# Latent attention on one core: the maxima's pieces moved between the scores, a narrower turn, and the gates applied after the heads

## The chip, the cores and the metric

The kernel runs on one core of a Trainium2 chip, in one launch. The metric is device time in microseconds (us), the median of several runs. The core's engines work side by side and wait for each other through semaphores: TensorE (PE in the profile, its weight loads PEld), VectorE (DVE), ScalarE (ACT), GpSimd (POOL) and SyncE (SP), which here issues nearly all DMAs. TensorE writes into PSUM, eight banks of 128 partitions by 512 float32.

## What is computed

The reference is a two-layer backbone: a layer of windowed attention, a layer of latent attention, and a last RMSNorm. There are 1024 latent tokens and 256 context tokens, so 1280 keys. The change touches the second layer only, from its attention on:

```python
s = (einsum("bqhd,bkhd->bhqk", qn, kn) + einsum("bqhd,bkd->bhqk", qr, kr)) * scale
p = softmax(s, axis=-1)
o = einsum("bhqk,bkhd->bqhd", p, v)          # 16 heads of 64
yx = (o * silu(gx)) @ w_out                  # the gate, then the output projection
x = x + gate_x * yx                          # then the final RMSNorm
```

## The kernel before

**Units.** The attention is cut into 16 units (`UnitB`, L1276; `NU = 16`): a unit is a pair of heads and one half (512) of the queries. Units 0 and 1 are the halves of pair 0, and so on. Its ten key tiles of 128 tokens are numbered c = 0 to 9.

**Scores and exponentials.** `score(c)` (L1332) multiplies key tile c with the unit's queries, keys on the partitions and 512 queries in the columns. The two heads lie in the two 64-row halves of the array and run side by side, so a "pair" of matmuls is two that overlap. There are five such pairs for each c: four with operands split into high and low parts (terms 0 to 3) and a fifth with 36 rows (term 4), in which four extra rows subtract the row maximum of each query. `score(c, i0, i1)` issues only terms i0 to i1. When the fifth is issued, ScalarE's exponential over both heads' banks follows (L1347), then an add of the result to a running sum (L1351, L1353; on GpSimd, and on VectorE for c > 4 of the last unit). The bank pair is 3,4 for even c and 5,6 for odd c, so S2, the scores of c = 2, can be written only when the exponential of c = 0 has read its banks. In what follows S2 is a tile's scores and E2 its exponential.

**Maxima.** Before unit u+1 can start, the row maxima of its scores must be known. They are taken from a rougher product with the queries on the partitions: `top(piece)` (L1297) issues four matmuls (eight of half the width for two of the ten pieces), and VectorE reduces each of two banks to a maximum (L1311, L1313). The ten pieces T0 to T9 of unit u+1 are issued within unit u. Their banks are 0, 1 and 2, taken in turn, two for a piece; so the second matmul of a piece waits for the reduction of the first bank of the piece before it. T4 and T9 are the two of eight matmuls.

**Turn and shift.** `turn` (L1315) reduces the pieces' maxima to one for each query and transposes them on TensorE, one 128-row by 100-column transpose (L1318). `shift` (L1320) writes them in diagonal form into the extra rows of the queries: for one head on VectorE (L1323), for the other as four ScalarE instructions (L1330).

**PV, and the end of a unit.** `PV` (L1355) multiplies the exponentials with the values, five key tiles at a time, into bank 7. `fin` copies the result out and loads the unit's gate; `fin2` adds the running sums over the partitions by a matmul with ones into bank 5 (L1371) and copies them out on ScalarE (L1373); `fin3(j)` takes the reciprocal of half the columns and multiplies (L1377, L1378); `fin4` multiplies with the gate and stores to DRAM (L1382, L1384). They run a unit late: unit u's `fin2` stands in unit u+1.

**Order.** In this part of the kernel the order on each engine is the order in which the program is written (`in_order`). For a unit the loop L1506 to L1556 issues:

```
S0 terms 0-3, S1 terms 0-3, T0, S0 term 4, T1, S1 term 4, S2, T2, S3, T3, S4, T4,
[fin2 of the last unit, PV of c = 0..4, fin3(0) of the last unit],
S5, T5, S6, T6, S7, T7, S8, T8, S9, T9, PV of c = 5..9, turn, fin3(1), shift, fin4, fill, fin
```

The fill is the next pair's keys (`make_K`, after units 0, 2, 4 up to 12), or the next four heads' values (`make_V`, after units 3, 7 and 11). After units 1, 5, 9, 13 and 14 there is none, so the next unit's S0 follows the turn at once.

**Queues.** SyncE's queue holds the loads of queries for the unit after next (`prep`, L1288), the gate's load, the stores of `fin4` and some loads of the output weights; it works in order too.

**Output tiles.** After the units, `out_tiles` (L1426) makes eight tiles of 128 tokens: 48 matmuls each (two halves of the columns, eight k-steps, three products: L126 to L128), four PSUM banks in turn. In tile t, after the first 24 matmuls, `cut_out` splits the attention output of tile t+1 into high (ScalarE, L121) and low part (VectorE, L122), and `fetch_out` (L1411) loads that of tile t+2. VectorE then multiplies with the layer's gate vector and adds x (L1447, L1448), ScalarE squares (L1449), GpSimd makes the root of the mean in three small instructions (L1459 to L1461), VectorE scales (L1472), SyncE stores (L1473). The first two fetches and the first cut stand in the last unit.

Of the kernel before, what the change touches and what calls it, by code (L numbers as in the profile page):

```python
# [22 lines left out]
NT = TOK // 128  # L23
# [36 lines left out]
def kernel(ctx: ExitStack, tc: tile.TileContext, t, out, dbg=None):  # L60
    nc = tc.nc
# [57 lines left out]
    def split(hi, lo, src, lo_eng=None):  # L119

        nc.scalar.copy(hi, src)  # L121
        (lo_eng or nc.vector).tensor_sub(lo, src, hi.bitcast(F32))  # L122
# [498 lines left out]
    units = [UnitA(ti, g) for ti in ORDER for g in range(4)]  # L621
# [43 lines left out]
    aw, xn, hs, w0 = {}, {}, {}, {}  # L665
# [201 lines left out]
    for bi, gp, c in order:  # L867
# [18 lines left out]
        r = proj_t(bi, gp, c)  # L886
# [22 lines left out]
    og = None  # L909
    fins = []  # L910
    for ui, u in enumerate(units):
# [248 lines left out]
    for ti in range(NT):  # L1160
        n = ti + 3
# [45 lines left out]
    NU = 16  # L1207
# [6 lines left out]
    glr = Ring(R, [30, 112], 512)  # L1214
# [61 lines left out]
    class UnitB:  # L1276
# [38 lines left out]
        def turn(self, bank):  # L1315
            nc.vector.reduce_max(shp(self.mx, 2, 64)[:, :, 32:36], self.mxp, AX.X, negate=True)
            self.pm = bank
            nc.tensor.transpose(self.pm[0:100, 0:128], self.mx[:, 0:100], ident)  # L1318

        def shift(self, engs):  # L1320
            for r, eng in zip((slice(32, 36), slice(96, 100)), engs):
                if eng is nc.vector:
                    eng.tensor_tensor(  # L1323
                        shp(self.q[r, 3], 4, 128), self.pm[r, 0:128].unsqueeze(1).to_broadcast([4, 4, 128]),
                        ident[r, r].unsqueeze(2).to_broadcast([4, 4, 128]), ALU.mult,
                    )
                else:
                    for b in range(4):
                        o = self.q[r, 3, b * 128 : b * 128 + 128]
                        eng.activation(o, self.pm[r, 0:128], AF.Copy, scale=ident[r, r.start + b : r.start + b + 1])  # L1330

        def score(self, c, i0=0, i1=5):  # L1332


            q, kt = self.q, self.kt
            cs = slice(c * 128, c * 128 + 128)
            b = 3 + 2 * (c % 2)
            terms = ((kt, 0, 0, 64), (kt, 0, 1, 64), (kt, 1, 0, 64), (KR, 0, 2, 64), (KR, 1, 3, 36))
            for i in range(i0, i1):
                k, s, sq, n = terms[i]  # L1340
                for e in range(2):
                    r = slice(64 * e, 64 * e + n)
                    nc.tensor.matmul(PB[:, b + e, :], k[r, s, cs], q[r, sq], start=i == 0, stop=i == 4)  # L1343
            if i1 < 5:
                return
            E = self.E[c] = shp(Er.next(), 2, 512)
            nc.scalar.activation(E, PB[:, b : b + 2, :], AF.Exp)  # L1347
            acc = shp(self.acc, 2, 512)
            eng = nc.vector if self.i == NU - 1 and c > 4 else nc.gpsimd
            if c == 1:  # L1350
                eng.tensor_add(acc, self.E[0], E)  # L1351
            elif c:
                eng.tensor_add(acc, acc, E)  # L1353
# [8 lines left out]
        def fin(self):  # L1362
            self.o = otr.next()
            nc.scalar.copy(self.o, PB[:, 7, :])
            self.gt = glr.next()
            load(out=self.gt.bitcast(F32), in_=g1_d[self.pair, :, self.ts])

        def fin2(self):
            acc = shp(self.acc, 2, 512)
# [2 lines left out]
            self.rec = self.acc[:, 0:512]  # L1372
            nc.scalar.copy(self.rec, psd)  # L1373

        def fin3(self, j):
            js = slice(256 * j, 256 * j + 256)
            nc.vector.reciprocal(self.rec[:, js], self.rec[:, js])  # L1377
            nc.vector.tensor_mul(self.o[:, js], self.o[:, js], self.rec[:, js])  # L1378
# [10 lines left out]
    ogl = Ring(R, [114, 118], 1024)  # L1389
    xr1 = Ring(R, [122, 126, 130], 1024)  # L1390
    yr = Ring(F, [26, 10, 14], 1024)
    junk1 = f_at(8, 256).bitcast(BF16)
# [16 lines left out]
                yield  # L1409

    def fetch_out(ti):  # L1411
        o = shp(ogl.next(), 8, 128)
        load(out=o.bitcast(F32), in_=og_d[:, :, ti * 128 : ti * 128 + 128].rearrange("c p n -> p c n"))
        x = xr1.next().bitcast(F32)
        load(out=x, in_=x1_d[256 + ti * 128 : 384 + ti * 128, :])
        return o, x

    def cut_out(f, eng=None):
        o, x = f
        og = shp(ogr1.next(), 2, 8, 128)  # L1420
        for h in range(2):
            hs = slice(4 * h, 4 * h + 4)
            split(og[:, 0, hs], og[:, 1, hs], o[:, hs].bitcast(F32), eng)
        return og, x

    def out_tiles(ready, got):  # L1426
# [66 lines left out]
    for b in range(4):  # L1493
        for i in range(3):
            units[0].top([(b, i)], (PB[:, 2 * i, :], PB[:, 2 * i + 1, :]))
        next(gs[b])
        next(gs[b])
        if b == 3:
            units[0].turn(psd)
            units[0].shift((nc.vector, nc.vector))  # L1500
# [5 lines left out]
    for ui, u in enumerate(units):  # L1506
        pu = units[ui - 1] if ui else None
        nu = units[ui + 1] if ui + 1 < NU else None
        nnu = units[ui + 2] if ui + 2 < NU else None
        for c in range(NT):  # L1510
            if c == 5:
                if pu:
                    pu.fin2()
                u.PV(0, 5)
                if pu:
                    pu.fin3(0)
                if pu and nu is None:
                    pu.fin4(0, 256)
                    first = fetch_out(0)
                    pu.fin3(1)  # L1520
                    pu.fin4(256, 512)
                    got = fetch_out(1)
            if c == 0:
                u.score(0, 0, 4)
                u.score(1, 0, 4)
            if c > 1:
                u.score(c)
            if nu:
                nu.top(PIECES[c])
            if c < 2:  # L1530
                u.score(c, 4, 5)
            if 0 < ui < 12 and c == 2 or ui == 6 and c == 7 or ui in (12, 13) and c in (2, 7):
                next(wo_fill, None)
            if nu is None and c == 0:
                load2(out=gx1, in_=gate_d[1, 0, :].partition_broadcast(128))
                load2(out=fg, in_=t["final_g"].partition_broadcast(128))
        if nnu:
            nnu.prep()
        u.PV(5, NT)
        if nu:  # L1540
            filled = u.half == 0 and u.pair < 7 or ui % 4 == 3
            nu.turn(psd if filled else topb())
            if pu:
                pu.fin3(1)
            nu.shift((nc.vector, nc.scalar))
            if pu:
                pu.fin4()
            fillb.i = topb.i
            fill = make_K(u.pair + 1) if u.half == 0 and u.pair < 7 else iter(())
            if ui % 4 == 3:  # L1550
                fill = make_V(ui // 4 + 1)
            for _ in fill:
                pass
        else:
            ready = cut_out(first)
        u.fin()  # L1556
    u.fin2()
    u.fin3(0)
    u.fin3(1)
    u.fin4()  # L1560
    out_tiles(ready, got)
    in_order.__exit__(None, None, None)

# [74 lines left out]
```

## Time and profile before

| | us |
|---|---|
| median of 3 runs | 1582.75 |
| lowest, highest | 1579.58, 1583.51 |
| the profiled execution's own time | 1582.15 |
| its span, first to last instruction | 1580.3 |
| TensorE busy in the span | 1522.8 |
| VectorE, GpSimd, ScalarE busy | 1015.2, 775.4, 734.9 |

The profile is of one execution. Rows of the timeline give start, duration, engine, line, operation, shapes, how many equal instructions were merged into the row, and in brackets the idle time before it with what ended it. A matmul's duration includes its way through the array (0.39 us for 512 columns), while the next starts 0.23 us later; so steps are read from start to start. The units lie between 1002.5 us (first turn) and 1485.8 us (first output matmul); the output tiles follow, to about 1573 us on TensorE.

### The profile page before, as it was taken

To read this page: it belongs to the slowest core of one execution; us is meant where nothing else is said; L and a number is where in the kernel's file an instruction comes from. 1 tells how busy PE (TensorE), PEld (TensorE's weight loads), DVE (VectorE), ACT (ScalarE), POOL (GpSimd) and SP (SyncE) were. 2 spreads that over 40 slices of the span, in tenths; PEclk is the share of its full clock that TensorE was granted. 3 is DMA by queue.
4 is the path that set the end of the run, shared out by engine and by line. 5 is a ranking of instruction groups with operands and counts; after the bars stand their busy time and mean duration, and the time that the engine had idled before them with its cause. 6 is when DMAs were issued, how large, how long until landed. Compare 5 with 4: busy or idle time off the path is not lost.

```text
span 1580.3 us, 24759 instructions
## 1 busy us (share of the span) xinstructions
PE 1522.8 (96%) x9026; PEld 1189.2 (75%) x9026; DVE 1015.2 (64%) x1895; ACT 734.9 (47%) x1433; POOL 775.4 (49%) x722
## 2 busy tenths in 40 slices
PE   6899999989999999998999999999999999999998
PEld 2788888778888888886987888766766666766687
DVE  2666868737767887777725202567678678677644
ACT  2512212238877777776523432344445444544422
POOL 2653446315554434444318340477677677688200
PEclk8999999989999999999999999999999999999999
DMA  8535644473333333316304841401122112111442
GB/s 301 175 118 183 196 144 171 144 223 108 114 111 94 97 94 94 94 55 222 92 16 145 308 129 54 117 15 50 44 68 71 44 44 87 44 45 37 140 160 80
DMA packets 123842, 178.91 MB, mean 113 GB/s; under 512 B 11708, under 2 KB 71996, under 8 KB 123720
## 3 DMA queue, kind: packets, MB, share of 16 engines
q1 hardware_dynamic: 116440, 166.40, 33.2%
q10 hardware_dynamic: 7280, 10.92, 2.3%
q8 instruction: 71, 1.16, 0.3%
q14 instruction: 51, 0.42, 0.1%
HBM read 131.13 MB, written 46.15 MB: 112 GB/s over the span
## 4 chain that ended last, share of the span: by engine, by line
PE 83%; DVE 5%; DMA 3%; POOL 3%; issue 3%; ACT 3%; SPq 0%; POOLq 0%; DVEq 0%; ACTq 0%
PE PB L126 14%; PE PB L127 13%; PE PB L128 13%; PE PB L1343 12%; PE PB L1360 9%; PE PB L1305 5%; PE PB L570 5%; PE PB L560 4%; PE PB L533 2%; PE PB L534 2%; PE PB L1371 1%; DMA arena_f<-a_w_in 1%; DMA arena_f<-x 1%; DVE arena_f L344 1%; POOL arena_r L122 1%
## 5 line engine op out<-in xcount | busy, mean ns | idle before, releaser
L126 PE MATMUL PB<-arena_r 128*128 128x512 f32 (+2 forms) x1312 | 475.7, 363 | 3.4 <-ACT arena_r L205 2.1
L127 PE MATMUL PB<-arena_r 128*128 128x512 f32 (+2 forms) x1312 | 469.5, 358 | 3.2 <-POOL arena_r L727 2.3
L128 PE MATMUL PB<-arena_r 128*128 128x512 f32 (+2 forms) x1312 | 469.2, 358 | 0.2 <-DVE arena_r L122 0.2
L1353 POOL TENSOR_TENSOR arena_f<-arena_f 128x1024 f32<-128x1024 f32 x123 | 294.6, 2395 | 18.8 <-ACT arena_f L1347 11.6
L126 PEld LDWEIGHTS PB<-arena_r 128*128 128x128 f32 x1312 | 250.4, 191 | 48.2 <-issue 6.9
L127 PEld LDWEIGHTS PB<-arena_r 128*128 128x128 f32 x1312 | 249.9, 191 | 37.8 <-POOL arena_r L727 2.8
L128 PEld LDWEIGHTS PB<-arena_r 128*128 128x128 f32 x1312 | 249.6, 190 | 35.4 <-DVE arena_r L122 0.4
L1311 DVE TENSOR_REDUCE krF<-PB 128x1 f32<-128x512 f32 (+1 forms) x264 | 167.2, 678 | 112.2 <-PE PB L1305 111.8
L1347 ACT ACTIVATE arena_f<-PB 128x1024 f32<-128x1024 f32 x160 | 164.3, 1027 | 157.2 <-PE PB L1343 154.5
L1343 PE MATMUL PB<-arena_r 64*128 64x512 f32 (+1 forms) x1600 | 220.0, 395 | 1.0 <-ACT arena_f L1347 0.9
L122 POOL TENSOR_TENSOR arena_r<-arena_f,arena_r 128x512 fp32r<-128x512 f32 x96 | 131.5, 1382 | 166.7 <-ACT arena_r L121 152.8
L1343 PEld LDWEIGHTS PB<-arena_r 64*128 64x128 f32 (+1 forms) x1600 | 159.4, 184 | 41.5 <-issue 13.3
L122 DVE TENSOR_TENSOR arena_r<-PB,arena_r 128x512 fp32r<-128x512 f32 (+2 forms) x215 | 140.1, 663 | 76.8 <-ACT arena_r L121 75.1
L540 DVE CUSTOM_DVE_ANT_0 arena_f<-PB,arena_f,small 128x256 f32<-128x256 f32 (+1 forms) x288 | 145.4, 524 | 32.6 <-PE PB L534 25.7
L121 ACT CAST arena_r<-PB 128x512 fp32r<-128x512 f32 (+2 forms) x215 | 120.0, 565 | 55.2 <-PE PB L560 40.9
L1360 PE MATMUL PB<-arena_f 128*64 128x512 f32 x640 | 143.6, 595 | 0.0
L541 ACT ACTIVATE arena_f<-arena_f,small 128x640 f32<-128x640 f32 (+2 forms) x160 | 118.9, 743 | 27.8 <-DVE small L540 26.7
L570 PE MATMUL PB<-arena_r 128*128 128x512 f32 x336 | 121.8, 438 | 4.7 <-ACT arena_f L581 4.1
L344 DVE SCALAR_TENSOR_TENSOR arena_f<-arena_f,small 128x512 f32<-128x512 f32 x98 | 116.2, 1232 | 3.9 <-DMA arena_f<-ada_w 3.5
L1305 PE MATMUL PB<-arena_r 64*128 64x512 f32 (+1 forms) x768 | 112.3, 360 | 6.5 <-DVE krF L1311 5.8
L1360 PEld LDWEIGHTS PB<-arena_f 128*64 128x64 f32 x640 | 44.4, 137 | 84.3 <-issue 82.0
L560 PE MATMUL PB<-ident,arena_f 128*128 128x128 f32 x672 | 105.8, 274 | 0.4 <-ACT arena_f L541 0.3
(165 smaller groups left out, 1892.8 us busy)
## 6 DMA issues: line engine op xcount, KB each, us to landing
arena_r<-q_d SPq DMA_DIRECT2D x148, 128.0 KB, 2.8
arena_f<-ada_w SPq DMA_DIRECT2D x64, 256.0 KB, 3.2
arena_f<-a_w_in SPq DMA_DIRECT2D x40, 256.0 KB, 3.0
arena_f<-ada_w SPq DMA_DIRECT2D x16, 512.0 KB, 7.2
arena_f<-x SPq DMA_DIRECT2D x16, 512.0 KB, 3.7
q_d<-arena_f SPq DMA_DIRECT2D x16, 512.0 KB, 3.2
qn_d<-arena_f SPq DMA_DIRECT2D x16, 512.0 KB, 5.7
arena_r<-qn_d SPq DMA_DIRECT2D x16, 512.0 KB, 5.8
```

Of the source, the lines that this page charges most:

```text
L122: (lo_eng or nc.vector).tensor_sub(lo, src, hi.bitcast(F32))
L126: nc.tensor.matmul(o, ah, bh, start=first, stop=False)
L127: nc.tensor.matmul(o, al, bh, start=False, stop=False)
L128: nc.tensor.matmul(o, ah, bl, start=False, stop=last)
L560: nc.tensor.transpose(pt[:, h, :], self.Ps[h][:, ci * 128 : ci * 128 + 128], ident)
L570: nc.tensor.matmul(self.pv, V[:, self.chunks[ci], self.g, :], PT[:, s], start=ci == 0 and s == 0, stop=ci == self.m - 1 and s == 1,)
L1305: nc.tensor.matmul(bank[:, o : o + n], self.q[r, s, bs], k[r, 0, n0 : n0 + n], start=s == 0, stop=s == 2)
L1311: nc.vector.reduce_max(self.mxp[:, e, b : b + 1, i], bank[:, 0:n], AX.X)
L1343: nc.tensor.matmul(PB[:, b + e, :], k[r, s, cs], q[r, sq], start=i == 0, stop=i == 4)
L1347: nc.scalar.activation(E, PB[:, b : b + 2, :], AF.Exp)
L1353: eng.tensor_add(acc, acc, E)
L1360: nc.tensor.matmul(PB[r, 7, :], Vq[:, c, h, :], E[:, e], start=c == 0, stop=c == NT - 1)
```

## The change

Parts, as they stand in the diff:

1. **The pieces of the maxima.** T0 stays behind S0 and S1. The fifth terms of S0 and S1 then follow each other directly. For c from 2 on, S(c) is cut at `CUT[c]` terms and T(c-1) stands in the cut; T9 follows S9. T4 so comes after the first PV.
2. **Turn.** Instead of one transpose of 100 columns, two matmuls of 64 columns each with the identity (L1319 of the changed kernel).
3. **Shift.** Both heads on VectorE. Its second reciprocal (`inv(1)`) comes before the shift, the multiply after it.
4. **Gates.** They are no longer multiplied in `fin4`. `fin3(j)` stores each half of a unit's columns as soon as it is multiplied. `fetch_out` loads the gates beside the attention output, and GpSimd multiplies the two (128 by 1024) for tiles 1 to 7; for tile 0 VectorE does it in `cut_out`.
5. **Last unit.** Three bank pairs for the scores (5,6; 3,4; 0,1), an exponential ring of five buffers in place of six, and the two constant vectors are loaded from SyncE's queue rather than ScalarE's.

With this the order of a unit is

```
S0 terms 0-3, S1 terms 0-3, T0, S0 term 4, S1 term 4, S2 terms 0-2, T1, S2 rest, S3 terms 0-1, T2, S3 rest,
S4 terms 0-1, T3, S4 rest, [fin2, PV of c = 0..4, inv(0), fin3(0)], S5 term 0, T4, S5 rest, S6 term 0, T5, S6 rest,
S7 term 0, T6, S7 rest, T7, S8, T8, S9, T9, PV of c = 5..9, turn, inv(1), shift, fin3(1), fill, fin
```

The core of the diff:

```diff
+    CUT = (4, 4, 3, 2, 2, 1, 1, 1, 0, 0)
...
-            nc.tensor.transpose(self.pm[0:100, 0:128], self.mx[:, 0:100], ident)
+            for r in HALF:
+                nc.tensor.matmul(self.pm[r, 0:128], self.mx[:, r], ident, start=True, stop=True)
...
-            b = 3 + 2 * (c % 2)
+            b = (5, 3, 0)[c % 3] if self.i == NU - 1 else 3 + 2 * (c % 2)
...
-            self.gt = glr.next()
-            load(out=self.gt.bitcast(F32), in_=g1_d[self.pair, :, self.ts])
...
-        def fin4(self, c0=0, c1=512):
-            cs = slice(c0, c1)
-            nc.vector.tensor_mul(self.o[:, cs], self.o[:, cs], self.gt[:, cs].bitcast(F32))
-            t0 = self.ts.start
-            load(out=og_d[self.pair, :, t0 + c0 : t0 + c1], in_=self.o[:, cs])
+        def inv(self, j):
+            js = slice(256 * j, 256 * j + 256)
+            nc.vector.reciprocal(self.rec[:, js], self.rec[:, js])
...
         def fin3(self, j):
             js = slice(256 * j, 256 * j + 256)
-            nc.vector.reciprocal(self.rec[:, js], self.rec[:, js])
             nc.vector.tensor_mul(self.o[:, js], self.o[:, js], self.rec[:, js])
+            t0 = self.ts.start + 256 * j
+            load(out=og_d[self.pair, :, t0 : t0 + 256], in_=self.o[:, js])
...
     def fetch_out(ti):
+        o, g = ogl.next(), ggl.next().bitcast(F32)
+        for dst, src in ((g, g1_d), (o, og_d)):
+            load(out=shp(dst, 8, 128), in_=src[:, :, ti * 128 : ti * 128 + 128].rearrange("c p n -> p c n"))
+        if ti:
+            nc.gpsimd.tensor_mul(o, o, g)
...
+            if gate:
+                nc.vector.tensor_mul(o[:, hs], o[:, hs], g[:, hs])
+            split(og[:, 0, hs], og[:, 1, hs], o[:, hs])
...
+            if c < 2:
+                u.score(c, 0, 4)
+            if c == 1:
+                if nu:
+                    nu.top(PIECES[0])
+                u.score(0, 4, 5)
+                u.score(1, 4, 5)
             if c > 1:
-                u.score(c)
+                u.score(c, 0, CUT[c])
+                if nu:
+                    nu.top(PIECES[c - 1])
+                u.score(c, CUT[c], 5)
...
             nu.turn(psd if filled else topb())
             if pu:
+                pu.inv(1)
+            nu.shift()
+            if pu:
                 pu.fin3(1)
-            nu.shift((nc.vector, nc.scalar))
-            if pu:
-                pu.fin4()
```

More of the change, by code (lines that the diff above doesn't have):

```diff
@@ L1213 @@
     accr = Ring(F, [44, 48], 1024)
-    glr = Ring(R, [30, 112], 512)
     otr = Ring(F, [0, 2], 512)
@@ L1317, in turn, with shift @@
             self.pm = bank
[L1318 to L1330, printed above, removed]
+            for r in HALF:
+                nc.tensor.matmul(self.pm[r, 0:128], self.mx[:, r], ident, start=True, stop=True)
+        def shift(self):
+            for r in (slice(32, 36), slice(96, 100)):
+                nc.vector.tensor_tensor(
+                    shp(self.q[r, 3], 4, 128), self.pm[r, 0:128].unsqueeze(1).to_broadcast([4, 4, 128]),
+                    ident[r, r].unsqueeze(2).to_broadcast([4, 4, 128]), ALU.mult,
+                )
         def score(self, c, i0=0, i1=5):
@@ L1411, in fetch_out, with cut_out @@
     def fetch_out(ti):
-        o = shp(ogl.next(), 8, 128)
-        load(out=o.bitcast(F32), in_=og_d[:, :, ti * 128 : ti * 128 + 128].rearrange("c p n -> p c n"))
+        o, g = ogl.next(), ggl.next().bitcast(F32)
[3 more added lines that the diff above has]
+            nc.gpsimd.tensor_mul(o, o, g)
+        o = shp(o, 8, 128)
         x = xr1.next().bitcast(F32)
         load(out=x, in_=x1_d[256 + ti * 128 : 384 + ti * 128, :])
-        return o, x
-    def cut_out(f, eng=None):
-        o, x = f
+        return o, x, shp(g, 8, 128)
+    def cut_out(f, gate=False):
+        o, x, g = f
         og = shp(ogr1.next(), 2, 8, 128)
@@ L1499 @@
             units[0].turn(psd)
-            units[0].shift((nc.vector, nc.vector))
+            units[0].shift()
         next(gs[b])
@@ L1506 @@
     for ui, u in enumerate(units):
+        if ui == NU - 1:
+            Er = Ring(F, [10 + 4 * c for c in range(5)], 1024)
         pu = units[ui - 1] if ui else None
@@ L1534 @@
             if nu is None and c == 0:
-                load2(out=gx1, in_=gate_d[1, 0, :].partition_broadcast(128))
-                load2(out=fg, in_=t["final_g"].partition_broadcast(128))
+                load(out=gx1, in_=gate_d[1, 0, :].partition_broadcast(128))
+                load(out=fg, in_=t["final_g"].partition_broadcast(128))
         if nnu:
@@ L1543 @@
             if pu:
+                pu.inv(1)
+            nu.shift()
+            if pu:
                 pu.fin3(1)
-            nu.shift((nc.vector, nc.scalar))
-            if pu:
-                pu.fin4()
             fillb.i = topb.i
@@ L1554 @@
         else:
-            ready = cut_out(first)
+            ready = cut_out(first, True)
         u.fin()
     u.fin2()
-    u.fin3(0)
-    u.fin3(1)
-    u.fin4()
+    for j in range(2):
+        u.inv(j)
+        u.fin3(j)
     out_tiles(ready, got)
```

14 lines of the change are left out of this document (4 added, 10 removed).

## The prediction

> **What bounds the kernel now.** I read the page first (busy shares), then the timeline of each engine within one unit, then the waits of the units' stretch.
>
> ```profile
> PE 1522.8 (96%) x9026; PEld 1189.2 (75%) x9026; DVE 1015.2 (64%) x1895; ACT 734.9 (47%) x1433; POOL 775.4 (49%) x722
> ```
>
> TensorE is busy nearly throughout, so an edit pays only where TensorE now waits. One unit (unit 10) on TensorE:
>
> ```profile
> 1308.59 0.32 PE L1318 MATMUL PB<-ident,krF 128*100 128x128 f32 x1
> 1308.84 2.11 PE L1343 MATMUL PB<-arena_r 64*128 64x512 f32 x16
> 1310.79 0.63 PE L1305 MATMUL PB<-arena_r 64*128 64x512 f32 x4
> 1311.26 0.39 PE L1343 MATMUL PB<-arena_r 36*128 36x512 f32 x2
> 1311.49 0.40 PE L1305 MATMUL PB<-arena_r 64*128 64x512 f32 x1
> 1312.20 0.72 PE L1305 MATMUL PB<-arena_r 64*128 64x512 f32 x3 [0.32 <-DVE krF L1311]
> 1312.54 1.78 PE L1343 MATMUL PB<-arena_r 36*128 36x512 f32 x12
> 1314.14 0.65 PE L1305 MATMUL PB<-arena_r 64*128 64x512 f32 x4
> 1314.61 1.33 PE L1343 MATMUL PB<-arena_r 64*128 64x512 f32 x10
> 1315.75 0.65 PE L1305 MATMUL PB<-arena_r 64*128 64x512 f32 x4
> ...
> 1317.36 0.67 PE L1305 MATMUL PB<-arena_r 64*128 64x256 f32 x8
> 1317.96 1.08 PE L1371 MATMUL PB<-arena_f,small 128*64 128x512 f32 x4
> 1318.87 4.46 PE L1360 MATMUL PB<-arena_f 128*64 128x512 f32 x20
> 1323.26 1.42 PE L1343 MATMUL PB<-arena_r 64*128 64x512 f32 x10
> ...
> 1331.53 4.51 PE L1360 MATMUL PB<-arena_f 128*64 128x512 f32 x20
> ```
>
> Start to start: a tile of scores takes 1.14 us (1314.61 to 1315.75, 0.229 a pair), a piece of maxima 0.47 (1314.14 to 1314.61), the piece of eight 0.6 (1317.36 to 1317.96). The first half (S0 to S4, T0 to T4) runs 1308.84 to 1317.96 = 9.12 us; the second, the same work, 1323.26 to 1331.53 = 8.27. So 0.85 us of a unit is waiting, all in its first half, around T1. What ended it:
>
> ```profile
> 1311.78 1.02 ACT L1347 ACTIVATE arena_f<-PB 128x1024 f32<-128x1024 f32 x1 [0.38 <-PE PB L1343]
> PE PB L1305 <- DVE krF L1311: 5.8, 15, 1.2
> ```
>
> T1's second matmul waits for the reduction of T0's first bank, 0.32 us here. The waits' row has it 15 times; less the longest (unit 14) that is 4.6 over 14, 0.33 each, so unit 10 stands for units 0 to 13. But a second wait hides behind the first: E0 ends at 1311.78 + 1.02 = 1312.80, and S2, which writes E0's banks, begins there (the row of twelve starts with S1's last matmul).
>
> **Part 1, the spread.** After the change S0's and S1's fifth terms follow T0, and S2 is next. S0's fifth starts at 1311.26 as now, E0 0.52 later, ends at 1312.80, and S2 can start 1.59 us after S0's fifth, as before. TensorE has 0.46 of work for these 1.59: it stands 1.13 us. T1, which used this time, comes later. From S2 on: 15 pairs of scores at 0.229 and three pieces at 0.465 are 4.83 us, so the first half ends 1.95 + 0.47 + 1.59 + 4.83 = 8.84 after its start, against 9.12: -0.28. The second half gains T4, the piece of eight: +0.58 to +0.60. Net **+0.31 us a unit**. Nothing else is queued behind that wait but T1 and S2's own exponential. No other wait appears: E1 ends 1.1 after E0, before S3 asks (1.6 after); each reduction pair (1.3 us) fits the 1.6 between pieces; T4's bank is long reduced. For 14 units: +4.3 us. Bounds: +0.16 (T4 costs 0.47 like the others) to +0.45.
>
> Unit 14 waits longer today:
>
> ```profile
> L1378 DVE TENSOR_TENSOR arena_f<-arena_f x32: 424/1458/2294, 1046.8 to 1490.5; 128x256 f32<-128x256 f32 x32
> 1432.51 2.11 PE L1343 MATMUL PB<-arena_r 64*128 64x512 f32 x16
> ...
> 1442.72 1.08 PE L1371 MATMUL PB<-arena_f,small 128*64 128x512 f32 x4
> ```
>
> The first row is the multiply with the reciprocal in all units (shortest, median, longest: 0.42, 1.46, 2.29 us), the others unit 14 on TensorE. Its first half is 10.21 us: the shift queues behind that multiply, and T0's reductions behind the gate's. Parts 3 and 4 put the shift ahead of the multiply and drop the gate's; it becomes an 8.84 like the others: 8.84 + 0.59 - 10.21 = **-0.8**. Elsewhere the gate's multiply, and its load, are off the path and worth nothing: T0's reduction is no longer what is late, E0 is.
>
> **Part 2 and 3, turn and shift.** Today's transpose takes 0.25 us to the next start (1308.59 to 1308.84), in the five turns with no fill. No row shows a product like the two new ones; the nearest is PV, 20 matmuls of 64 columns by 512 in 4.39 (1318.87 to 1323.26), so 0.44 a pair and a quarter of that, 0.11, for 128 columns. So two products in place of one transpose may cost 0.11 instead of 0.25, or 0.25 each. I take 0.03 more a turn over 15 turns, near the lower end, since the two use separate halves of the array as PV's do: **+0.5**; the ends are -2.1 (0.14 less on each) and +3.8 (0.25 more). The shift is two small VectorE instructions, on both heads; S0's fifth asks 2.67 us after the turn (1311.26 - 1308.59), and VectorE has nothing else then, the reciprocal being done during PV (4.39): covered even at 1 us each.
>
> **Part 5, the last unit.**
>
> ```profile
> 1460.98 2.73 PE L1343 MATMUL PB<-arena_r 64*128 64x512 f32 x20
> 1464.65 4.05 PE L1343 MATMUL PB<-arena_r 64*128 64x512 f32 x30 [0.95 <-ACT arena_f L1347]
> ...
> 1473.94 6.66 PE L1343 MATMUL PB<-arena_r 64*128 64x512 f32 x50
> 1480.52 4.51 PE L1360 MATMUL PB<-arena_f 128*64 128x512 f32 x20
> ...
> 1485.82 0.50 PE L126 MATMUL PB<-arena_r 128*128 128x512 f32 x1
> ```
>
> Here S2 behind two fifth terms does wait 0.95 us for E0: the pattern that part 1 makes everywhere else, seen in the trace. Three bank pairs remove it. An exponential (1.02 and the step between two) then just keeps pace with a tile of scores at 1.14, so nearly all of the wait goes (-0.9). The second takes 5.7 to 5.9 (25 pairs at 0.229, and the step from PV), not 6.58 (-0.7). **-1.6**. The two constants' loads on SyncE cost nothing: its queue in that unit holds only what part 4 counts, half a unit later. The cut of tile 0 (two more VectorE multiplies) just fits, since VectorE's adds for this unit start earlier without the two gate multiplies ahead of them; if they don't, -0.5.
>
> **Part 4, the output tiles.** A tile is 48 matmuls at 0.227 us, 10.88 us, the step from one fetch to the next (1513.28 to 1524.16). First the fourth tile's GpSimd, VectorE and SyncE rows and its DMA rate (last column, GB/s), then two earlier fetches, with the first one's cut:
>
> ```profile
> 1521.15 0.19 POOL L1459 TENSOR_TENSOR small<-small 128x1 f32<-128x1 f32 x1 [9.78 <-ACT arena_f L1449]
> 1522.29 1.42 DVE L1472 SCALAR_TENSOR_TENSOR arena_f<-arena_f,small 128x512 f32<-128x512 f32 x2 [2.03 <-POOL small L1461]
> 1513.28 0.41 SPq L1413 DMA_DIRECT2D arena_r<-og_d  x1
> 1524.16 0.41 SPq L1413 DMA_DIRECT2D arena_r<-og_d  x1
> 1527.20:1527.70 0.50, 0.50 (x3) 0.39 (x3) 0.00 (x0) 0.00 (x0) 0.00 (x0) 1.00 1.23 405
> 1477.61 0.37 SPq L1413 DMA_DIRECT2D arena_r<-og_d  x1
> 1483.42 1.14 ACT L121 CAST arena_r<-arena_r 128x512 fp32r<-128x512 f32 x2 [1.71 <-DMA arena_r<-og_d]
> 1492.08 0.37 SPq L1413 DMA_DIRECT2D arena_r<-og_d  x1
> L1353 POOL TENSOR_TENSOR arena_f<-arena_f 128x1024 f32<-128x1024 f32 x123 | 294.6, 2395 | 18.8 <-ACT arena_f L1347 11.6
> ```
>
> A ring closes: GpSimd's product of tile t+2 stands ahead of its three small instructions of tile t; these release VectorE's scaling, this SyncE's store, and the next fetch stands behind the store. From the fetch's issue the attention output alone is there after 3.5 us at the earliest (by 1527.70 the rate is 405 GB/s, that of x's long rows behind it) and 5.8 at the latest (1477.61 to 1483.42, among other transfers); I take 4.1, nearer the undisturbed one. The gates ahead of it are as much data again: 1.3 us (0.52 MB at 405 GB/s) to 3.5; I take 2.2. So the landing is 6.3 us after the issue. The product 2.4, GpSimd's three 1.1, to the next issue 1.9 (1522.29 to 1524.16): 11.7 a round against 10.88, so each fetch is issued 0.84 later in its tile than the last. The first is issued 7.4 us into tile 0 (today 1492.08 - 1485.82 = 6.3; plus 0.7 for the multiplies in the cut less the gate's, plus 0.4 for the second store; both estimates, the first from L1378's shortest row, the second from a SyncE issue of 0.41). TensorE waits when the cut misses the tile: issue + 6.3 + 2.4 + 1.1 + 2.1 (scaling and first low part) over 2 x 10.88 + 0.2, so from an issue of 10.1 on. The sixth fetch stands at 7.4 + 5 x 0.84 = 11.6: **+1.5 us**. With a landing x later the cost is 1.5 + 6x (five rounds and the deadline): nothing up to 6.05, +11.7 at 8.0 (5.8 + 2.2), +19.5 at the far end, 5.8 + 3.5.
>
> By the Trainium skill, SBUF — State Buffer, section Who interferes with whom, a VectorE instruction with two inputs in SBUF and a GpSimd instruction that reads SBUF block each other for a whole instruction. The row of L1378 above, 0.42 at the shortest and 2.29 at the longest beside GpSimd's adds, agrees. By that rule tile 1's product could hold the last unit's multiply by up to 2 us, the first fetch would be issued at 9.4, and the drift would cost 3.5: 1588.1.
>
> **The sum.** +4.3 - 0.8 + 0.5 - 1.6 + 1.5 = +3.9 on the profiled execution's 1582.15 (span 1580.3 and 1.85 around it): **1586.1 us**. That execution lies 0.6 under the median of 1582.75. A measurement of this kernel tells about 0.3% (4.75 us) from no change.
>
> **Rivals.** *Faster: S2 doesn't stand for E0.* Then the first half takes 8.84 - 1.13 = 7.71, the second 0.59 more than now, and a unit saves 0.82: -11.5 for 14 units, -1.9 for unit 14, the rest as above: 1569. For it: the waits of T1 do go. Against: S2 starts within 0.05 us of E0's end in unit 10, and waits for it in the last unit. It would need E0 to end 1.1 us earlier than any row has it. *The spread nets nothing:* T4 costs nothing in its new place, the rest stands: 1582. *Slower: the gated fetch sets the output tiles' pace.* From a landing of 6.05 us on, each 0.1 more costs 0.6 us over the six fetches; at 8.0, 1596. For it: two transfers of short rows one behind the other, and the store ahead of the fetch. Against: the 5.8 was tile 0's, among four other transfers.
>
> **How the numbers follow.** Forecast 0.55 (its own range 1583 to 1590), nets nothing 0.15, slower rival 0.20, faster rival 0.10. The range 1581 to 1594 takes in the first two with their bounds and half of the third; it leaves out the faster rival and the far half of the slower. Against 1582.75: slower by over 0.3% (above 1587.5) is the slower rival and four tenths of the forecast, 0.42; faster by over 0.3% is the faster rival, 0.11; within 0.3%, 0.47.
>
> **What would show it.** Right: in each unit TensorE idle for about 1.1 us at S2 with ScalarE's exponential as releaser, none at T1 for VectorE; first halves 8.8, second 8.85; the last unit 23.2 from its first score to the first output matmul (now 1460.98 to 1485.82, 24.8); L121 or L122 in the output tiles ever later, and TensorE waiting for them in tiles 6 and 7 alone. Wrong: no wait at S2; turns of over 0.3 us; output tiles of over 11.5 us from the third on.

## The result, and the profile after

| | before | after |
|---|---|---|
| median of 5 runs, us | 1582.57 | 1597.73 |
| lowest, highest | 1579.58, 1583.51 | 1594.75, 1599.19 |
| the profiled execution's own time, its span | 1582.15, 1580.3 | 1594.75, 1593.0 |
| first turn to last turn (units 0 to 14) | 458.3 | 469.4 |
| last turn to first output matmul | 25.1 | 23.3 |
| output tiles, first matmul to start of the last | 87.4 | 91.4 |

The changed kernel is slower by 0.97% (ratio 1.0097, 95% interval 1.008 to 1.0113). The prediction said 1586.1, its range ended at 1594. The stages of the profiled executions add up: +11.1 - 1.8 + 4.0, and 0.7 less ahead of the first turn, make 12.6; the spans differ by 12.7. The medians differ by 15.2. The profiled execution of the changed kernel is the lowest of its five, and no trace shows what made the others longer.

TensorE's share hardly moves. The page's first row of the changed kernel, and from the waits of its units (us in total, times, longest) the only row in which TensorE itself waits:

```profile
PE 1524.7 (96%) x9074; PEld 1195.0 (75%) x9074; DVE 982.7 (62%) x1895; ACT 715.7 (45%) x1373; POOL 791.1 (50%) x729
```

```profile
PE PB L1339 <- ACT arena_f L1343: 14.2, 15, 1.0
```

T1's wait for VectorE is gone from the list; in its place the scores (now L1339) wait for the exponential (L1343), about 0.95 us in each of 15 units. Unit 10 on TensorE, and E0 with E1 on ScalarE:

```profile
1316.40 2.11 PE L1339 MATMUL PB<-arena_r 64*128 64x512 f32 x16
1318.36 0.63 PE L1305 MATMUL PB<-arena_r 64*128 64x512 f32 x4
1318.82 0.63 PE L1339 MATMUL PB<-arena_r 36*128 36x512 f32 x4
1320.42 0.98 PE L1339 MATMUL PB<-arena_r 64*128 64x512 f32 x6 [0.97 <-ACT arena_f L1343]
1321.23 0.63 PE L1305 MATMUL PB<-arena_r 64*128 64x512 f32 x4
1321.70 1.10 PE L1339 MATMUL PB<-arena_r 64*128 64x512 f32 x8
1322.64 0.73 PE L1305 MATMUL PB<-arena_r 64*128 64x512 f32 x4
...
1324.76 0.92 PE L1339 MATMUL PB<-arena_r 64*128 64x512 f32 x6
1325.61 1.08 PE L1365 MATMUL PB<-arena_f,small 128*64 128x512 f32 x4
...
1330.91 0.50 PE L1339 MATMUL PB<-arena_r 64*128 64x512 f32 x2
1331.24 0.65 PE L1305 MATMUL PB<-arena_r 64*128 64x256 f32 x8
1331.73 1.33 PE L1339 MATMUL PB<-arena_r 64*128 64x512 f32 x10
...
1339.87 4.51 PE L1356 MATMUL PB<-arena_f 128*64 128x512 f32 x20
```

```profile
1319.34 1.94 ACT L1343 ACTIVATE arena_f<-PB 128x1024 f32<-128x1024 f32 x2 [2.45 <-PE PB L1339]
```

S0's fifth term starts at 1318.82, E0 at 1319.34, S2 at 1320.42: 1.60 us behind the fifth, as predicted (1.59). But the first half takes 1325.61 - 1316.40 = 9.21, not 8.84, and the second 1339.87 - 1330.91 = 8.96, not 8.86.

The last unit, with three bank pairs, runs its first fifty score matmuls without a gap (6.39 from their start to `fin2`, 7.65 before), the second fifty in 5.99 (6.58 before):

```profile
1471.50 6.17 PE L1339 MATMUL PB<-arena_r 64*128 64x512 f32 x50
1477.89 1.08 PE L1365 MATMUL PB<-arena_f,small 128*64 128x512 f32 x4 [0.22 <-ACT arena_f L1343]
...
1483.19 6.06 PE L1339 MATMUL PB<-arena_r 64*128 64x512 f32 x50
1489.18 4.51 PE L1356 MATMUL PB<-arena_f 128*64 128x512 f32 x20
...
1494.48 0.50 PE L126 MATMUL PB<-arena_r 128*128 128x512 f32 x1
```

In the output tiles (numbered from 0), four of the gates' six fetches on SyncE with GpSimd's products, the sixth among them, then the matmuls that wait in tiles 4 and 7:

```profile
1501.73 0.43 SPq L1408 DMA_DIRECT2D arena_r<-g_d  x1
...
1513.60 0.44 SPq L1408 DMA_DIRECT2D arena_r<-g_d  x1
...
1526.31 0.39 SPq L1408 DMA_DIRECT2D arena_r<-g_d  x1
...
1561.87 0.42 SPq L1408 DMA_DIRECT2D arena_r<-g_d  x1
```

```profile
1508.28 2.40 POOL L1410 TENSOR_TENSOR arena_f<-arena_f,arena_r 128x1024 f32<-128x1024 f32 x1 [9.34 <-DMA arena_f<-og_d]
1510.63 0.19 POOL L1459 TENSOR_TENSOR small<-small 128x1 f32<-128x1 f32 x1
...
1520.84 2.39 POOL L1410 TENSOR_TENSOR arena_f<-arena_f,arena_r 128x1024 f32<-128x1024 f32 x1 [9.10 <-DMA arena_f<-og_d]
...
1569.36 2.39 POOL L1410 TENSOR_TENSOR arena_f<-arena_f,arena_r 128x1024 f32<-128x1024 f32 x1 [9.40 <-DMA arena_f<-og_d]
```

```profile
1538.88 0.50 PE L127 MATMUL PB<-arena_r 128*128 128x512 f32 x1 [0.34 <-DVE arena_r L122]
...
1574.91 0.50 PE L127 MATMUL PB<-arena_r 128*128 128x512 f32 x1 [1.67 <-DVE arena_r L122]
```

The product starts when the fetch has landed, 6.55 and 7.24 us after its issue, and the three small instructions stand behind it; the next fetch follows 11.87 and 12.71 after the last, while a tile is 10.88. The sixth product starts 7.49 after its fetch. From tile 4 on TensorE waits: tiles 4 to 6 take 11.55 to 11.58 each, and tile 7 takes 13.04 (11.07 before), so half of the 4.0 us is the one wait at the start of tile 7.

### The profile page after: what moved, and what is told of

Its sections match the earlier page's. It is cut to its first block, busy times and chain, and to the rows that moved or that the text cites. A ratio compares the mean times of both kernels' runs of the same rounds, so it can differ in the third digit from the quotient of the medians.

```text
span 1593.0 us, 24884 instructions
## 1 busy us (share of the span) xinstructions
PE 1524.7 (96%) x9074; PEld 1195.0 (75%) x9074; DVE 982.7 (62%) x1895; ACT 715.7 (45%) x1373; POOL 791.1 (50%) x729
## 3 DMA queue, kind: packets, MB, share of 16 engines
q8 instruction: 71, 1.16, 0.3%
## 4 chain that ended last, share of the span: by engine, by line
PE 77%; DVE 6%; DMA 5%; POOL 4%; ACT 4%; issue 3%; SPq 0%; POOLq 0%; ACTq 0%; DVEq 0%
PE PB L126 12%; PE PB L1339 12%; PE PB L127 11%; PE PB L128 11%; PE PB L1356 8%; PE PB L1305 5%; PE PB L570 5%; PE PB L560 4%; PE PB L533 2%; DMA arena_f<-og_d 2%; PE PB L534 2%; ACT arena_f L1343 1%; DVE arena_f L344 1%; PE PB L1365 1%; POOL arena_f L1410 1%
## 5 line engine op out<-in xcount | busy, mean ns | idle before, releaser
L1343 ACT ACTIVATE arena_f<-PB 128x1024 f32<-128x1024 f32 x160 | 162.2, 1026 | 185.4 <-PE PB L1339 184.8
L1339 PE MATMUL PB<-arena_r 64*128 64x512 f32 (+1 forms) x1600 | 227.6, 397 | 14.2 <-ACT arena_f L1343 14.2
L122 POOL TENSOR_TENSOR arena_r<-arena_f,arena_r 128x512 fp32r<-128x512 f32 x96 | 131.8, 1385 | 167.0 <-ACT arena_r L121 155.3
L1339 PEld LDWEIGHTS PB<-arena_r 64*128 64x128 f32 (+1 forms) x1600 | 164.7, 185 | 53.4 <-ACT arena_f L1343 21.2
L122 DVE TENSOR_TENSOR arena_r<-PB,arena_r 128x512 fp32r<-128x512 f32 (+2 forms) x215 | 140.1, 663 | 77.6 <-ACT arena_r L121 76.7
L121 ACT CAST arena_r<-arena_f 128x512 fp32r<-128x512 f32 (+1 forms) x136 | 78.9, 608 | 96.7 <-POOL arena_f L1410 29.4
L1305 PE MATMUL PB<-arena_r 64*128 64x512 f32 (+1 forms) x768 | 110.0, 359 | 0.7 <-DVE arena_r L122 0.7
```

Of the source, the lines that this page charges most:

```text
L1305: nc.tensor.matmul(bank[:, o : o + n], self.q[r, s, bs], k[r, 0, n0 : n0 + n], start=s == 0, stop=s == 2)
```

## The experiments

Totals scatter with the code ahead of the units (the first turn lies between 999 and 1004 us in these profiles), so the stages decide, and the medians confirm. Stages in us, as in the table above; ratios to the kernel before, with 95% intervals.

| run | median | ratio | units | last unit | tiles |
|---|---|---|---|---|---|
| order_back | 1588.39 | 1.0038 (1.0018 to 1.0058) | 460.5 | 23.3 | 91.4 |
| t1_first | 1590.58 | 1.0055 (1.004 to 1.0071) | 461.5 | 23.3 | 96.2 |
| ring_open | 1591.33 | 1.0056 (1.0041 to 1.0071) | 469.6 | 23.3 | 87.4 |
| turn_whole | 1591.03, one run | | 467.9 | 23.2 | 91.9 |
| cuts_none | 1587.46 | 1.0027 (1.0017 to 1.0038) | 459.6 | 23.3 | 94.8 |
| t4_first | 1600.18 | 1.0114 (1.01 to 1.0128) | 473.3 | 23.3 | 92.1 |
| two_pairs | 1599.4, one run | | 469.6 | 25.0 | 94.6 |
| spread_only | 1591.59 | 1.0057 (1.0042 to 1.0073) | 468.2 | 25.0 | 87.4 |
| order_only | 1573.51 | 0.9945 (0.9931 to 0.9958) | 450.0 | 25.1 | 87.4 |
| best | 1569.33 | 0.9919 (0.9905 to 0.9933) | 447.9 | 23.2 | 87.4 |

The theory: S2 stands for E0 because nothing is left to do behind S0's fifth; T4 leaves a step behind when it moves; and the ring in the output tiles turns slower than a tile.

### order_back: part 1 undone

```diff
-            if c < 2:
-                u.score(c, 0, 4)
-            if c == 1:
-                if nu:
-                    nu.top(PIECES[0])
-                u.score(0, 4, 5)
-                u.score(1, 4, 5)
+            if c == 0:
+                u.score(0, 0, 4)
+                u.score(1, 0, 4)
             if c > 1:
-                u.score(c, 0, CUT[c])
-                if nu:
-                    nu.top(PIECES[c - 1])
-                u.score(c, CUT[c], 5)
-            if nu and c == NT - 1:
+                u.score(c)
+            if nu:
                 nu.top(PIECES[c])
+            if c < 2:
+                u.score(c, 4, 5)
```

> The changed kernel with the earlier order of the maxima's pieces (part 1 undone, the rest stays). Theory A (TensorE now stands at S2 for E0 with nothing to do, and T4 left a mode switch and a restart behind): the units, first turn to last turn, go from 469.4 us back to about 459, and the time is about 1587. Rival B (the shift on VectorE alone or the two-product turn delays the units, whatever the order): the units stay at 466 or more, the time at 1594 or more.

The units came to 460.5, 8.9 less than in the changed kernel. A holds, B falls: with the old order the turn, the shift and the gates cost 2.3 us together.

### spread_only: part 1 alone, on the kernel before

The same lines as above, the other way round, and CUT.

> The kernel before with part 1 alone, the spread pieces. Theory A (E0's wait is laid bare and T4 leaves its step behind; the turn, the shift and the gates have no part in it): 0.65 us more in each of units 0 to 13, unit 14 by itself no more or a little less, so the units go from 458.3 us to about 467 and the time is 8 to 9 above the kernel before, about 1591. The prediction's size for the same part (0.31 a unit, less 0.8 in unit 14): units at 462, time 3.5 above.

The turn's row (instructions, durations, first and last start) gives the units:

```profile
L1319 PE MATMUL PB<-ident,krF x16: 270/316/316, 1002.2 to 1470.4; 128*100 128x128 f32 x16
```

468.2 us, 9.9 more than before: 0.71 a unit in units 0 to 13 (0.62 to 0.82), and unit 14 at 28.53 against 28.47. The spread alone makes the kernel 9.2 us slower in the median. A holds; the prediction's size was less than half of it.

### t1_first: T1 directly ahead of S2

```diff
-    CUT = (4, 4, 3, 2, 2, 1, 1, 1, 0, 0)
+    CUT = (4, 4, 0, 2, 2, 1, 1, 1, 0, 0)
```

> The changed kernel with T1 directly ahead of S2 (cut 0 in place of 3 for c = 2); all other pieces stay spread. Theory A (S2 waits for E0): T1's 0.47 us falls into the stall and each of 15 units gets shorter by about that, so the units take about 462.4 us in place of 469.4 and the time is about 1590.7. Rival C (the cost lies in cutting the scores and switching between them and the maxima, and S2's wait is a by-product): one cut fewer of nine, so 1.5 us at most.

Units 461.5: 7.9 us less for moving one piece. Units 0 to 13 lose 0.58 each in the mean; unit 14 gets 0.18 longer, since T1 waits 0.9 there for T0's reductions. So A holds for 14 of its 15 units, and C falls. In unit 10:

```profile
1315.60 0.63 PE L1339 MATMUL PB<-arena_r 36*128 36x512 f32 x4
1316.07 1.20 PE L1305 MATMUL PB<-arena_r 64*128 64x512 f32 x4
1317.20 0.50 PE L1339 MATMUL PB<-arena_r 64*128 64x512 f32 x2
```

S2 starts 1.60 behind S0's fifth with T1 in front of it, as it did without: T1's 0.47 fell wholly into the wait. The rest of it, 0.66, now shows inside T1's row (1.20 long, where 0.63 is usual), since T1's second matmul again starts only when T0's first reduction has ended, and S2 starts with the end of E0; so TensorE's list of waits names neither, but for T1 in unit 14. The median is the expected one; the profiled execution, 1593.97, is the longest of four, with 4.8 us more in the tiles, whose code nothing had touched (see "Left open").

### cuts_none: whole tiles between the pieces

```diff
-    CUT = (4, 4, 3, 2, 2, 1, 1, 1, 0, 0)
+    CUT = (4, 4, 0, 0, 0, 0, 0, 0, 0, 0)
```

> The changed kernel with every cut at 0: the pieces stand between whole tiles of scores, T1 ahead of S2, T4 still behind the first PV. Against the run with T1 alone moved it undoes the cuts of S3 to S7 and nothing else. Theory A (a cut costs little by itself: each step of five pairs that holds one took 1.16 to 1.18 us in place of 1.14, and a skew of up to 0.1 us between the two heads' matmuls is lost where the tile shape changes): 0.1 to 0.2 us a unit, the units 458.5 to 460, the time about 1587. Rival C (a cut accumulation group is itself expensive): 0.4 us a unit or more, the units at 455.5 or less.

Units 459.6, against 461.5: 0.12 a unit for five cuts. Cutting a group of scores costs little; C falls.

### t4_first: T4 back ahead of the first PV

```diff
-                if nu:
+                if nu and c != 5:
                     nu.top(PIECES[c - 1])
                 u.score(c, CUT[c], 5)
+                if nu and c == 4:
+                    nu.top(PIECES[4])
```

> The changed kernel with T4, the piece of eight, back ahead of the first PV; the rest stays spread. Theory A (T4 itself is 0.48 us; 0.12 of the 0.60 it showed before is the step to matmuls of another shape, which the scores pay when T4 is gone): the first half grows from 9.15 by about 0.48, the second shrinks from 8.93 to about 8.3, so 0.15 a unit and the units go from 469.4 to about 467. The prediction's view (T4 is 0.60 in the first half and 0.59 in the second): no change within 0.5 us.

Missed by both: the units went up, to 473.3. The second half shrank by 0.47, what T4 is worth; the first grew by 0.72. T4 now stands only three pairs behind T3, and its second bank is T3's first:

```profile
1326.04 0.70 PE L1305 MATMUL PB<-arena_r 64*128 64x512 f32 x4
1326.50 0.92 PE L1339 MATMUL PB<-arena_r 64*128 64x512 f32 x6
1327.20 0.98 PE L1305 MATMUL PB<-arena_r 64*128 64x256 f32 x8
1328.11 1.08 PE L1365 MATMUL PB<-arena_f,small 128*64 128x512 f32 x4
```

```profile
1326.70 1.29 DVE L1311 TENSOR_REDUCE krF<-PB 128x1 f32<-128x512 f32 x2 [0.36 <-PE PB L1305]
```

T3's first reduction ends at 1326.70 + 0.65 = 1327.35, while T4 starts at 1327.20; T4 to the next step is 0.91 where 0.60 was usual, 0.31 lost. The step before it is 0.70 again (0.85 in the changed kernel), so the part of the theory about the step at the change of tile shape holds; the placing added a wait that neither view had counted. T3's first bank comes free 1.31 us after T3's start, and T4 started 1.16 after it.

### turn_whole: the turn in one transpose again

```diff
-            for r in HALF:
-                nc.tensor.matmul(self.pm[r, 0:128], self.mx[:, r], ident, start=True, stop=True)
+            nc.tensor.transpose(self.pm[0:100, 0:128], self.mx[:, 0:100], ident)
```

> The changed kernel with the one transpose of 100 columns in place of the two 64-column products; the shift stays on VectorE. Theory A: the step of the ten turns with a fill behind them goes from 3.98 back to 3.71 us and the PV ahead of it from 4.34 to 4.44, so about 1.5 us in all over the units. Rival E (it is the shift, now VectorE's alone, that stretches these steps): they stay at 3.98.

Units 467.9, 1.57 less; the ten steps with a fill are back at 3.71 (7.43 with the values' fill, which had been 7.70), the PV at 4.44. A holds, and E falls.

### two_pairs: the last unit with two bank pairs

```diff
-            b = (5, 3, 0)[c % 3] if self.i == NU - 1 else 3 + 2 * (c % 2)
+            b = 3 + 2 * (c % 2)
```

> The changed kernel with two bank pairs (3,4 and 5,6) for the scores of the last unit, as in all others. Theory A (the third pair is what took the last unit's waits away): last turn to first output matmul goes from 23.3 us back to 25.0, all of it before the two PVs. Rival F (the gain came from the gates' multiplies that went): it stays at 23.3 to 23.6.

```profile
1471.52 2.57 PE L1339 MATMUL PB<-arena_r 64*128 64x512 f32 x20
1475.07 4.04 PE L1339 MATMUL PB<-arena_r 64*128 64x512 f32 x30 [0.98 <-ACT arena_f L1343]
```

25.0 us, and S2's wait for the exponential is back, the very row of the units. The wait goes with the bank pair, so it is the banks that S2 waits for. A holds, and F falls.

### ring_open: GpSimd's product behind its three small instructions

```diff
-        if ti:
-            nc.gpsimd.tensor_mul(o, o, g)
+        raw = o, g
...
+            if ti < 6:
+                gate_out(got)
```

(`gate_out` holds the product; the second call stands in `out_tiles`, behind the three small instructions of tile ti; tile 1's product stands in the last unit as before.)

> The changed kernel with GpSimd's product of gates and attention output issued behind the three small instructions of the tile, not ahead of them; the units are untouched. Theory A (in the output tiles a ring closes over the product, the small instructions, the store and the next fetch): the tiles, first to last matmul, go from 91.4 us to between 87.5 and 88.5, the time to about 1594. Rival D (the product holds VectorE up by its use of SBUF, wherever it stands in GpSimd's queue): they stay at 90 or more.

```profile
1502.97 0.43 SPq L1408 DMA_DIRECT2D arena_r<-g_d  x1
...
1512.31 0.45 SPq L1408 DMA_DIRECT2D arena_r<-g_d  x1
...
1525.48 0.39 SPq L1408 DMA_DIRECT2D arena_r<-g_d  x1
...
1536.32 0.40 SPq L1408 DMA_DIRECT2D arena_r<-g_d  x1
```

The third and fourth issue are 10.84 apart, a tile's length; the tiles are back at 87.4. The product costs nothing in the new place, with the same fetches and the same VectorE work beside it: the ring is the cause, and D falls.

### order_only and best: another order

In both, a unit begins so (the rest as in the kernel before, the last unit's S0 and S1 with their fifths behind both):

```diff
+            elif c == 0:
+                u.score(0, 0, 4)
+                nu.top(PIECES[0])
+                u.score(0, 4, 5)
+            else:
+                u.score(c)
+                if nu:
+                    nu.top(PIECES[c])
```

`order_only` is the kernel before with this alone; `best` is the changed kernel with this, the one transpose and the open ring.

> The kernel before with the order of the first pieces alone changed (S0 terms 0 to 3, T0, S0's fifth, S1, T1, S2, and so on; in the last unit S0, S1, then the fifths as in the changed kernel); turn, shift on VectorE and ScalarE, gates, banks and output tiles as before. Theory A (the order is what pays, the other parts are small): units behind a fill lose 0.7 to 0.85 us, the three later units without one 0.2 to 0.5 (the shift on two engines ends 2.2 us after the turn, 0.6 after S0's fifth could start), the units about 449, the last unit and the tiles as before, 25.1 and 87.7, the time about 1573. Rival G (it needs the shift on VectorE alone, the multiply behind the shift and the gates gone from the units): units at 455 or more, time at 1579 or more.

> A version meant to beat both: in each unit S0 terms 0 to 3, T0, S0's fifth term, S1, T1, S2, T2 and so on to S4, T4, then the PV and the second half as before; the last unit's order, banks and loads as changed; the turn in one transpose; GpSimd's gate product behind the tile's three small instructions. Theory A (E0's 1.54 us behind S0's fifth term are covered by S1 and T1, 1.6 us, so S2 does not stand): the units behind a fill lose the whole 0.85 us of waiting in their first half, the five without a fill 0.2 to 0.5 of it, since S0's fifth then comes up to the shift's end; units about 448, last unit 23.3, tiles 87.7; the time about 1570. Rival C (cuts and switches, not E0): the units at 456 or more, the time at 1578 or more.

Units 450.0 and 447.9, medians 1573.51 and 1569.33, close to what was expected. From the page of `best`, the scores' row (its last column is the idle time of TensorE ahead of them), and a unit without a fill from its S0 on:

```profile
L1338 PE MATMUL PB<-arena_r 64*128 64x512 f32 (+1 forms) x1600 | 217.5, 394 | 0.0
```

```profile
1299.16 1.19 PE L1338 MATMUL PB<-arena_r 64*128 64x512 f32 x8
1300.19 0.62 PE L1305 MATMUL PB<-arena_r 64*128 64x512 f32 x4
1300.65 1.76 PE L1338 MATMUL PB<-arena_r 36*128 36x512 f32 x12
1302.04 0.64 PE L1305 MATMUL PB<-arena_r 64*128 64x512 f32 x3
```

S0's fifth, S1 whole and T1 are 1.39 + 0.47 = 1.86 us of work from the start of the fifth on, more than the 1.6 that E0 needs. The order alone brings 8.3 us in the units, more than all parts of the change that help. It is not complete: in `order_only` units 7 and 13 lose only 0.10 and 0.14 us where the other units behind a fill lose about 0.8. T0 takes 1.32 and 1.28 there (0.62 is usual), and the waits put it down to VectorE's last reads of the fill's results (L122). Of the 4.2 us between the two medians, 1.8 is in the last unit, with its third bank pair, and 2.1 is in the units; no run tells which part brings those 2.1.

## Why the prediction was wrong

S2's wait for E0 and the ring in the output tiles came as forecast, and their sizes were too small; for unit 14 the cause was wrong as well. Step by step, predicted and measured:

| step | predicted | measured | from |
|---|---|---|---|
| part 1 | +4.3 | +9.9 | spread_only against before |
| unit 14 | -0.8 | -0.4 | unit 14, 28.08 against 28.47 |
| turn | +0.5 | +1.6 | turn_whole against the changed kernel |
| last unit | -1.6 | -1.8 | two_pairs: 1.7 of it the banks |
| output tiles | +1.5 | +4.0 | ring_open |
| sum | +3.9 | +13.3 | |

The 0.7 us less ahead of the first turn brings this to the 12.6 of the profiled executions.

**Part 1, the step that failed most.** S2's wait for E0 came as described and as long; T1's wait was gone. Two prices were wrong. First, "the first half ends 8.84 after its start" let T4 take all its 0.60 along. By itself it is 0.49 (1331.24 to 1331.73 in unit 10 after); the rest was the step to the next matmuls, of another tile shape, and the scores pay it now: S4's last three pairs take 0.85 to `fin2`, not 0.69, and an uncut S4 1.26, not 1.14 (`cuts_none`, unit 10). By the Trainium skill, TensorEngine Tiling (Array Packing), section Key Properties, a change of the tiling mode drains TensorE; the trace agrees, with 0.12 here. Second, 15 pairs were put at 0.229 each, though a stall does not end at full pace: S2's first three pairs take 0.81, 0.12 more. The rest is cut steps, after which the second head's matmuls run up to 0.10 behind the first's: T2's row of four lasts 0.73 where 0.63 is usual. Together 9.21 - 8.84 = 0.37 a unit, and about 0.1 in the second half. The bounds of +0.16 to +0.45 moved T4's price alone and took the pace of full rows for granted (with T4 at 0.47 the lower one is -0.28 + 0.47 = +0.19). What the prediction did not draw was the conclusion in its own numbers: a piece fits S2's wait whole, so spreading away from it is a loss, and filling it better would be a gain.

**Turn.** Two readings failed. PV's row of twenty was taken for twenty matmuls; the code issues ten there (five key tiles, two heads), and each shows as two records. Read so, the two products come at 0.22 and not at 0.11, and the change of shape behind them adds about 0.10. And the 0.25 of today's transpose was read from the turns without a fill and used for all 15, though ten have a fill behind them. One of those in the kernel before, then in the changed one:

```profile
1335.97 0.32 PE L1318 MATMUL PB<-ident,krF 128*100 128x128 f32 x1
1336.05 0.48 PE L126 MATMUL PB<-arena_r 128*128 128x512 f32 x1
```

```profile
1344.22 0.39 PE L1319 MATMUL PB<-ident,krF 128*64 128x128 f32 x4
1344.54 0.50 PE L126 MATMUL PB<-arena_r 128*128 128x512 f32 x1
```

A transpose over 100 columns is followed by the fill after 0.08, the products (four records for two) after 0.32. The PV ahead ends 0.10 earlier, since the products have its shape. That is a net +0.17 on the ten turns with a fill and -0.03 on the four without one. Unit 0's turn, which other 128x128 matmuls follow, costs 0.34 more as well. Together this is 1.9; `turn_whole` shows 1.57, since its second halves are 0.03 a unit longer than the changed kernel's, which no run explains.

**Unit 14.** It does lose its long first half (10.21 to 9.20), but to the real 9.2 and not to 8.84, and not by parts 3 and 4 alone. `order_back` has both without part 1, and there the half is still 10.18. With the gate's multiply gone and the shift ahead, the multiply with the reciprocal stands right ahead of T0's reductions; it takes 2.10 us beside a GpSimd add (1436.30 to 1438.69), and T1 waits longer than before (1.41 against 1.17):

```profile
1436.87 2.10 DVE L1375 TENSOR_TENSOR arena_f<-arena_f 128x256 f32<-128x256 f32 x1
```

```profile
1439.74 0.73 PE L1305 MATMUL PB<-arena_r 64*128 64x512 f32 x3 [1.41 <-DVE krF L1311]
```

`spread_only` has part 1 without the two, and the half is 9.57. So most of the gain comes from moving T1 away from T0, and parts 3 and 4 help only then.

**Last unit.** Right, and shown to be the banks.

**Output tiles.** The ring closed where it was said to, the first fetch went out 7.25 into tile 0 (said 7.4). The landing was the mis-sized term: where 6.3 was taken, the first five fetches landed 6.2 to 7.2 after their issue, 6.65 in the mean, and the sixth 7.49. So a round took 12.03 in the mean and not 11.7, which makes 1.5 over five rounds, and the sixth fetch reached tile 7's matmuls after 13.04 and not 11.9, which makes another 1.1. With the predicted 1.5, and 0.15 less for the earlier first fetch, this is the measured 4.0. "The gated fetch sets the pace", listed as the slower rival, half happened. By the Trainium skill, SBUF — State Buffer, section Who interferes with whom, VectorE's multiply with two inputs could have been held by tile 1's product, which would have put the first fetch at 9.4. That product (1496.53 to 1498.93) met one of the two multiplies; this one took 0.69 us, the other, alone, 0.42. So the overlap cost 0.3 at most, and the rule was not what decided here.

**The rivals.** The faster one, that S2 doesn't stand for E0, falls by 15 waits in a row, by t1_first and by two_pairs. "The spread nets nothing" falls by spread_only (its 1582 needs a net of zero a unit; with a T4 that costs nothing, as its text has it, the sum would be about 1577). Two signs of being wrong came true: turns of 0.32, and output tiles of over 11.5, though only from tile 4 on. All errors but the last unit's had one sign: the terms were built from matmuls at full pace and from early landings. The range had room for the ring, but not for part 1 at twice its size.

**Left open.** With the same code the tiles took 91.4 to 96.2 us in the seven profiles with the closed ring (87.4 in all five without): products began between 6.1 and 8.3 us after their fetch's issue. Part of the scatter is TensorE's clock. In three of the seven the granted clock falls to half for 3.4 us just after TensorE has waited 1.8 to 2.0 us in tile 4 or 7 (`t1_first` twice, `cuts_none` and `two_pairs` once). Matmuls then start 0.43 us apart and not 0.23, which costs about 1.6 us each time. For `t1_first` (the last three columns are the granted clock, the DMA share and GB/s):

```profile
1536.50:1539.80 3.30, 3.30 (x9) 2.54 (x8) 2.37 (x4) 1.45 (x4) 0.00 (x0) 0.50 0.90 243
```

In the changed kernel's profile, `order_back` and `t4_first` waits of 1.7 to 1.9 us were not followed by this. Why the landings, and the clock after such a wait, differ from run to run is not shown.

## What to carry to other kernels

When one wait ends, look at who stands behind it and when its own release comes: here a second one, for the exponential, ended just as T1 did, and the piece that seemed to suffer from the first wait was the cover of the second. Place filler by the length of each wait (1.6 us behind S0's fifth) and not evenly, and keep two uses of a buffer as far apart as its readers need. In an in-order queue, an instruction that waits for a DMA belongs behind those whose results release the next DMA.

## What the runs showed of the hardware

- A change of the matmuls' tile shape cost 0.10 to 0.12 us on TensorE at three places (S4 to `fin2`, 1.26 against 1.14; the first pair of scores behind PV, 0.33 against 0.23; PV to the transpose, 4.44 against 4.34 to the products of PV's own shape); the first pair after a stall lost as much (0.34 against 0.23).
- A float32 matmul of PV, of `fin2` and of the turn's products shows as two records; a row of twenty is ten matmuls.
- The two 64-column float32 products of the turn show as four records and took 0.32 us to the next matmul; one 100-column transpose took 0.08 before a 128x128 matmul and 0.25 before a 64x128 one.
- Five cuts in the accumulation groups of a unit cost 0.12 us in all.
- Of seven waits of TensorE of 1.67 to 1.96 us in the output tiles, four were followed by 3.4 us at half the granted clock (waits of 1.82, 1.88, 1.94 and 1.96 us), three were not (1.67, 1.83 and 1.91).
